# Low parts of the MLP's weights: an accumulating transfer in place of GpSimd's subtraction

## The chip, the cores and the metric

The kernel runs on one core of one Trainium2 chip. The metric is device time in microseconds (us) of one execution; the time before is the median of 2 runs. The engines are named as in the profile: PE (TensorE matmul) and PEld (its weight loads), DVE (VectorE), ACT (ScalarE), POOL (GpSimd) and SP (SyncE). A letter q behind an engine (SPq) stands for its queue, from which transfers are issued.

## What is computed

The reference is one block of a hybrid encoder over 512 tokens and 16 meta tokens (528 in all), 1024 features: a stick-breaking attention and a gated linear attention in parallel, merged by gates, and then a gated MLP with a causal depthwise convolution of width 3. The change touches the MLP alone:

```python
hn = _rmsnorm(h, norm_ffn_pre[l])
up = hn @ w_ffn_up[l]                                   # 1024 x 2816
act = gelu(_causal_dwconv(up, conv_w[l], conv_b[l]))
ffn = (act * (hn @ w_ffn_gate[l])) @ w_ffn_down[l]      # 2816 x 1024
h = h + _rmsnorm(ffn, norm_ffn_post[l])
```

All of it is float32. The kernel multiplies in the format fp32r, which keeps fewer bits, and so each float32 operand x is split exactly into a high part hi (x rounded to fp32r) and a low part lo = x - hi. A product is then three matmuls: hi times hi, hi times lo and lo times hi.

## The kernel before

**Order.** The kernel is written with tiles in named pools. A planner puts the instructions of each engine into one fixed order, by its own estimate of when each can run; on the chip an engine takes its instructions in that order, and each waits for semaphores of the others. SP issues all weight loads from one queue, in order. `issue_after` adds a dependency by hand.

**Weight blocks.** `load_w` (lines 79 to 90) brings one block of at most 1024 weights a partition, 512 KB: SP loads it into `raw` (line 83), ACT rounds it into the high part (line 88), and an engine, POOL unless the call says otherwise, subtracts to give the low part (line 89). The pool `wp` has three `raw` tiles, and two tiles each for the high and the low part (`wh`, `wl`). A caller can give another pool for these two with `into`, or its own places with `hi_out` and `lo_out`.

**The MLP's first half** (lines 922 to 941). A loop over m runs over 22 blocks of 128 of the 2816 columns. Each turn does one up block (`proj`, lines 98 to 110: 8 blocks of rows, three products each, in two column ranges of the tokens), the convolution and GELU on ACT and DVE, one gate block (lines 933 to 939, 24 matmuls of 512 columns), and the split of the product into `fh` and `fl`. Even m take the places of `wp`, odd m those of a second pool, `wx`: four places for 44 weight blocks. For the first two m the two column ranges are apart, so that PE can begin with the tokens that are normed first, and the gate blocks are tied by hand to a step of the norm (`late`, line 932).

**The stage ahead of it** (lines 804 to 915) is the output projection `wo`, its norm, the residual, the second norm and the transposes into `h2h` and `h2l`, one token tile at a time. ACT does squares, rstd steps and the high parts of `h2`; DVE does the gains and half of the low parts, POOL the other half (line 842, through line 204). The loads and splits of the first MLP blocks lie beside it.

**The MLP's second half** (lines 947 to 1006). `down(0, 512, ...)` multiplies `fh` and `fl` with the first 512 columns of the down weights, in blocks of two row blocks, and `down(512, 256, ...)` with the next 256, four row blocks at a time; both go through `wp`. The last 256 columns are loaded whole (lines 988 to 991), in six blocks of four row blocks (the last has two), into `wdh` and `wdl`, and the token tiles then go through them one after the other (lines 993 to 998), so that each tile's final norm and output (lines 999 to 1006) lie beside the next tile's matmuls. In the profile the three are named d, dq and e.

Of the kernel before, what the change touches and what calls it, by code (L numbers as in the profile page):

```python
# [13 lines left out]
ALU = mybir.AluOpType  # L14
# [35 lines left out]
def block_kernel(ctx: ExitStack, tc: tile.TileContext, x, meta_tokens, norm_mix_pre, w_in, w_gk_up, b_gk,  # L50
# [22 lines left out]
    def f32(ap):  # L73
        return ap.bitcast(F32)

# [1 line left out]
    last_raw = [None]  # L77

    def load_w(src, nk, name, hi_out=None, lo_out=None, lo_eng=pool, into=None):
        """A block of at most 1024 weights a partition, and its exact split into two 12-bit parts."""  # L80
        ncol = src.shape[-1]
        raw = wp.tile([P, nk, ncol], F32, tag="raw", name=f"raw_{name}")
        sp.dma_start(raw, src)
        last_raw[0] = raw
        if hi_out is None:
            hi_out = (into or wp).tile([P, nk, ncol], F32R, tag="wh", name=f"wh_{name}", bufs=2)
            lo_out = (into or wp).tile([P, nk, ncol], F32R, tag="wl", name=f"wl_{name}", bufs=2)
        act.copy(hi_out, raw)  # L88
        lo_eng.tensor_tensor(out=lo_out, in0=raw, in1=f32(hi_out), op=ALU.subtract)  # L89
        return hi_out, lo_out  # L90
# [7 lines left out]
    def proj(w, xh, xl, segs, name, apart=False):  # L98
        """Feature-major product over two neighbouring column ranges of xh + xl, in two neighbouring banks."""
        wh, wl = w  # L100
        nk, m = wh.shape[1], wh.shape[2]
        (l0, l1), (_, l2) = segs
        pt = mmt(f"pt_{name}")
        segs = [(pt[:m, 512 - l1 + l0 : 512], l0, l1), (pt[:m, 512 : 512 + l2 - l1], l1, l2)]
        steps = [(k, a, b) for k in range(nk) for a, b in ((wh, xh), (wh, xl), (wl, xh))]
        for grp in ([[s] for s in segs] if apart else [segs]):
            for n, (k, a, b) in enumerate(steps):
                for dst, lo, hi in grp:
                    pe.matmul(dst, a[:, k, :], b[:, k, lo:hi], start=n == 0, stop=n == len(steps) - 1)  # L109
        return pt[:m, 512 - l1 + l0 : 512 + l2 - l1]  # L110
# [3 lines left out]
    def rstd_of(pl, ss, n, name, between=None):  # L114
        """(ss / n + eps) ** -0.5 with a Newton step."""
        shp = list(ss.shape)
        r0 = pl.tile(shp, F32, tag=f"rs_r{shp[1]}", name=f"r0_{name}")
        act.activation(r0, ss, AF.Ln, scale=1.0 / n, bias=epst[: shp[0]])
        last_exp[0] = act.activation(r0, r0, AF.Exp, scale=-0.5)
        v = pl.tile(shp, F32, tag=f"rs_v{shp[1]}", name=f"v_{name}")  # L120
        dve.tensor_scalar(out=v, in0=ss, scalar1=-0.5 / n, scalar2=-0.5 * EPS, op0=ALU.mult, op1=ALU.add)
        if between:
            between()
        a = pl.tile(shp, F32, tag=f"rs_a{shp[1]}", name=f"a_{name}")
        if shp[1] == 1:
            dve.tensor_scalar(out=a, in0=v, scalar1=r0, scalar2=r0, op0=ALU.mult, op1=ALU.mult)
        else:
            dve.tensor_tensor(out=a, in0=r0, in1=r0, op=ALU.mult)
            dve.tensor_tensor(out=a, in0=a, in1=v, op=ALU.mult)
        dve.scalar_tensor_tensor(out=a, in0=a, scalar=1.5, in1=r0, op0=ALU.add, op1=ALU.mult)  # L130
        return a
# [9 lines left out]
    def tables(n):  # L141
        """The activation table set that the next functions are in."""
        return act.add_instruction(mybir.InstLoadActFuncSet(
            act_func_set_id=n, name=nc.get_next_instruction_name(), engine=mybir.EngineType.Activation, ins=[], outs=[]))

    def sigmoid(pl, x, m, nm, bufs=1, tag="lse", out=None):
        """exp(min(x, 0) - ln(1 + exp(-|x|))); m is room for the minimum, or None to read x for it late."""
        e = pl.tile(list(x.shape), F32, tag=tag, name=f"lse{nm}", bufs=bufs)
        act.activation(e, x, AF.Abs)
        if m is not None:  # L150
            dve.tensor_scalar(out=m, in0=x, scalar1=0.0, scalar2=None, op0=ALU.min)
        act.activation(e, e, AF.Exp, scale=-1.0)
        act.activation(e, e, AF.Ln, bias=1.0)
        if m is not None:
            dve.tensor_tensor(out=e, in0=m, in1=e, op=ALU.subtract)
        else:
            dve.scalar_tensor_tensor(out=e, in0=x, scalar=0.0, in1=e, op0=ALU.min, op1=ALU.subtract)
        out = e if out is None else out
        act.activation(out, e, AF.Exp)
        return out  # L160

# [14 lines left out]
    # -1 where row >= column  # L176
# [8 lines left out]
    # =================== normalized input, feature-major, in two parts ===================  # L185
# [13 lines left out]
    def split_g(pl, hi, lo, src, g, nm, lo_eng=dve):  # L199
        """Both parts of src, a block of features after the other, with a gain by feature."""  # L200
        y = pl.tile([P, *src.shape[1:]], F32, tag="yg", name=f"yg{nm}", bufs=4)
        last_yg[0] = dve.tensor_tensor(out=y, in0=src, in1=g.unsqueeze(2).broadcast_to(list(src.shape)), op=ALU.mult)
        last_hi[0] = act.copy(hi, y)
        return lo_eng.tensor_tensor(out=lo, in0=y, in1=f32(hi), op=ALU.subtract)  # L204

    def diagonal(pl, r, n, nm):
        """r on the diagonal: a product with it transposes and scales by token."""
# [4 lines left out]
    with tc.tile_pool(name="p0", bufs=2, side="right") as p0:  # L212
        xts = {i: p0.tile([P, D], F32, name=f"xt{i}", bufs=1) for i in range(1, 5)}
        # the meta tokens, a partition for each block of 128 features, and the gain likewise
# [7 lines left out]
        def warm(n, nm):  # L222
            """Keeps the array's clock up while the first tokens are on their way."""
# [64 lines left out]
        # convolution taps and bias, and the second gain, by feature  # L288
# [40 lines left out]
    # =================== gated linear attention ===================  # L329
    with ExitStack() as pgs:  # L330
        pgc = pgs.enter_context(tc.tile_pool(name="pgc", bufs=1))
        # masks: level masks by compressed query, and the diagonal
# [27 lines left out]
        # log forget gates, token-major  # L360
# [62 lines left out]
        def gla(h, k, q, vT):  # L423
            # cumulative log decay inside chunks
# [12 lines left out]
            # pairs inside a chunk, by the block halves that part them: both factors decay  # L437
            def factors(lv, n, kt):
                """Keys of the first halves of the blocks, in place, and queries of the second halves, packed."""
# [45 lines left out]
            # values, token-major  # L485
# [12 lines left out]
            # queries with the decay since the chunk began, keys with the decay to its end  # L498
# [77 lines left out]
    # =================== stick-breaking attention ===================  # L576
# [4 lines left out]
    with tc.tile_pool(name="pa", bufs=1) as pa:  # L581

        def sb_parts(j, k, q, v):
            """Both parts of a head's keys stacked, against each part of its queries twice; values with both parts side by side."""
# [21 lines left out]
        def logits(dst, w, hd, ks, qs, st):  # L606
            """dst += (k_hi + k_lo).T (q_hi + q_lo)."""
# [3 lines left out]
        def softplus(z, n, rows, nm, i):  # L611
            """softplus of z, in PSUM."""
# [29 lines left out]
        def passed(nm, vp, rows, n, cs, tag):  # L642
            """exp of the sum over a whole key block, for each query, on all partitions."""
# [7 lines left out]
        def sb(j, ks, qh, ql, vs):  # L651
# [3 lines left out]
            # the first and the last 16 tokens: [16, head, (first, last), 16]  # L655
# [13 lines left out]
            # keys 384..511  # L669
# [17 lines left out]
            # out of the first 16 queries  # L687
# [5 lines left out]
            def add_halves(hd, src, t0, n):  # L693
                """The products with both parts of the values, added up."""
# [58 lines left out]
        def gate_sb(j):  # L753
            """A gate, kept where the high part of what it gates will be."""
# [8 lines left out]
    # =================== gates and output projections ===================  # L763
# [3 lines left out]
    # the last two meta tokens: too few for the array, their products are summed over the blocks of 128 rows first  # L767
# [26 lines left out]
    # =================== mixed output, residual, norm ===================  # L794
# [9 lines left out]
    with tc.tile_pool(name="pw", bufs=1) as pw:  # L804
# [7 lines left out]
        def gained(i, pt, hf):  # L812
            """Half of the mixed output of a tile with the gain, and its sum of squares."""
# [12 lines left out]
        def normed(i):  # L826
            """Residual, second norm, and both parts of the result by feature."""
# [16 lines left out]
        def mini():  # L844
            """The same for the last two meta tokens, by feature from the start."""
# [30 lines left out]
        # the first half of the columns for all tokens, then the second one token tile at a time  # L876
# [41 lines left out]
    # =================== gated MLP with the causal convolution ===================  # L918
# [3 lines left out]
    with tc.tile_pool(name="pu", bufs=2) as pu:  # L922
        for m in range(FT):
            pt = proj(load_w(cols(w_up, m * P), KT, f"up{m}", into=wx if m % 2 else None), h2h, h2l, FFNS, f"up{m}", apart=m < 2)
# [7 lines left out]
            with tc.issue_after(late.ins) if m < 2 else ExitStack():  # L932
                wh, wl = load_w(cols(w_gate, m * P), KT, f"ga{m}", into=wx if m % 2 else None)
# [12 lines left out]
    # =================== down projection, norm, residual ===================  # L946
    with tc.tile_pool(name="pd", bufs=1) as pd:
# [40 lines left out]
        for k0 in range(0, FT, 4):  # L988
            nk = min(4, FT - k0)
            load_w(w_down[k0 * P : (k0 + nk) * P, 768:].rearrange("(k p) m -> p k m", p=P), nk, f"e{k0}",  # L990
                   hi_out=wdh[:, k0 : k0 + nk, :], lo_out=wdl[:, k0 : k0 + nk, :])
# [40 lines left out]
```

## Time and profile before

| what | us |
|---|---|
| median of 2 runs (984.88 and 985.22) | 985.05 |
| span of the profiled execution | 983.2 |
| PE busy in it | 958.5 |
| DVE, ACT, POOL busy | 558.8, 461.5, 401.2 |
| first half of the MLP alone on PE | about 626 to 853 |
| second half, to the last matmul | about 853 to 977 |

The profile is one execution, taken by the hardware profiler. Times in the rows of its timeline are us from the start of the span, then the duration, the engine, the line, the operation, the tile written, the tiles read, the shapes and the count of merged instructions; in brackets stands how long the engine sat idle before, and what ended it. The rows of busy time by stretches have the stretch and its length, then busy us (and instruction counts) of PE, PEld, DVE, ACT and POOL, the granted clock of TensorE (1.00 is full), the share of the transfer engines' time, and GB/s. Rows of transfers have the count, the size and the median time from issue to landing. An engine's idle time costs nothing where it is not what the others wait for.

### The profile page before, as it was taken

How to read it: one execution, taken by the hardware profiler on the slowest of the kernel's cores; microseconds unless marked ns; L12 is line 12 of the kernel's file. 1: busy time of each engine (PE TensorE's matmuls, PEld its weight loads, DVE VectorE, ACT ScalarE, POOL GpSimd, SP SyncE). 2: the span in 40 equal slices, each digit the busy share in tenths (PEclk: the TensorE clock that was granted, in tenths of full speed). 3: DMA queues.
4: the chain of work that ended last, by engine and by line, in shares of the span. 5: the costliest groups of instructions: out<-in, count | busy, mean ns of one | idle time of the engine just before them, and what ended most of it. 6: DMA issues, size and time to landing. Idle time of an engine off the chain costs nothing.

```text
span 983.2 us, 17022 instructions
## 1 busy us (share of the span) xinstructions
PE 958.5 (97%) x6918; PEld 895.8 (91%) x6918; DVE 558.8 (57%) x970; ACT 461.5 (47%) x868; POOL 401.2 (41%) x285
## 2 busy tenths in 40 slices
PE   7999999999999998999999899999999999999997
PEld 7999999999999998999998779999988999888997
DVE  6675867767547786787849957444343444300112
ACT  5664645545467574676663244533333333311331
POOL 5523232222244454454545433543443443243460
PEclk9999999999999999999999899999999999999999
DMA  7122221222222222222223441333323323223231
GB/s 212 45 65 65 65 55 54 65 66 60 67 58 72 71 65 65 65 65 66 72 58 112 153 144 43 100 95 91 103 86 92 102 86 95 78 86 102 82 117 65
DMA packets 127552, 81.28 MB, mean 83 GB/s; under 512 B 3680, under 2 KB 120162, under 8 KB 127474
## 3 DMA queue, kind: packets, MB, share of 16 engines
q1 hardware_dynamic: 126082, 76.00, 27.0%
q10 hardware_dynamic: 1392, 4.19, 1.1%
q8 instruction: 54, 0.88, 0.4%
q14 instruction: 24, 0.20, 0.1%
HBM read 78.09 MB, written 2.10 MB: 82 GB/s over the span
## 4 chain that ended last, share of the span: by engine, by line
PE 85%; DVE 8%; issue 2%; ACT 2%; POOL 1%; DMA 1%; SPq 1%; DVEq 0%; POOLq 0%; ACTq 0%
PE pt_up L109 13%; PE ga L938 12%; PE d L965 6%; PE pt_gr L109 5%; PE pt_gv L109 5%; PE pt_go L109 4%; PE pt_mg L109 4%; PE e L998 3%; PE dq L965 3%; PE pt_gk L109 2%; PE pt_sv L109 2%; PE wo L887 2%; PE pt_ms L109 2%; PE pt_gq L109 2%; PE pt_sk L109 2%
## 5 line engine op out<-in xcount | busy, mean ns | idle before, releaser
L89 POOL TENSOR_TENSOR wl_up<-raw_up,wh_up 128x1024 fp32r<-128x1024 f32 x22 | 52.9, 2406 | 70.8 <-ACT wh_up L88 70.8
L89 POOL TENSOR_TENSOR wl_ga<-raw_ga,wh_ga 128x1024 fp32r<-128x1024 f32 x22 | 52.6, 2393 | 56.6 <-ACT wh_ga L88 56.6
L929 DVE SCALAR_TENSOR_TENSOR cy<-pt_up,cw,cy 128x511 f32<-128x511 f32 (+1 forms) x44 | 32.8, 746 | 74.1 <-ACT cy L926 74.1
L109 PE MATMUL pt_up<-h2l,wh_up 128*128 128x256 f32 (+1 forms) x352 | 73.6, 283 | 0.3 <-DVE h2l L204 0.2
L109 PE MATMUL pt_up<-h2h,wh_up 128*128 128x256 f32 (+1 forms) x352 | 73.5, 283 | 0.0
L109 PE MATMUL pt_up<-h2h,wl_up 128*128 128x256 f32 (+1 forms) x352 | 73.3, 282 | 0.0
L938 PE MATMUL ga<-h2l,wh_ga 128*128 128x512 f32 (+1 forms) x192 | 72.2, 376 | 0.0
L938 PE MATMUL ga<-h2h,wl_ga 128*128 128x512 f32 (+1 forms) x192 | 72.1, 375 | 0.0
L938 PE MATMUL ga<-h2h,wh_ga 128*128 128x512 f32 (+1 forms) x192 | 72.1, 376 | 0.0
L89 POOL TENSOR_TENSOR wl_d<-raw_d,wh_d 128x1024 fp32r<-128x1024 f32 (+1 forms) x17 | 39.6, 2332 | 63.7 <-ACT wh_d L88 63.7
L88 ACT CAST wh_up<-raw_up 128x1024 fp32r<-128x1024 f32 x22 | 23.0, 1050 | 85.6 <-PE pt_up L109 76.2
L135 DVE TENSOR_TENSOR fl<-cy,fh 128x512 fp32r<-128x512 f32 x22 | 50.2, 2282 | 15.1 <-ACT fh L134 15.1
L109 PEld LDWEIGHTS pt_up<-h2h,wh_up 128*128 128x128 f32 x352 | 56.9, 189 | 1.7
L109 PEld LDWEIGHTS pt_up<-h2l,wh_up 128*128 128x128 f32 x352 | 55.5, 189 | 0.7 <-DVE h2l L204 0.7
L109 PEld LDWEIGHTS pt_up<-h2h,wl_up 128*128 128x128 f32 x352 | 55.4, 189 | 0.0
L88 ACT CAST wh_d<-raw_d 128x1024 fp32r<-128x1024 f32 (+1 forms) x17 | 17.5, 1029 | 65.8 <-PE d L965 45.1
L940 DVE TENSOR_TENSOR cy<-ga,cy 128x512 f32<-128x512 f32 x22 | 15.2, 691 | 49.0 <-PE ga L938 47.9
L938 PEld LDWEIGHTS ga<-h2h,wl_ga 128*128 128x128 f32 x192 | 36.2, 188 | 7.0
L938 PEld LDWEIGHTS ga<-h2l,wh_ga 128*128 128x128 f32 x192 | 36.2, 188 | 6.2
L938 PEld LDWEIGHTS ga<-h2h,wh_ga 128*128 128x128 f32 x192 | 36.2, 188 | 6.1
L974 DVE TENSOR_TENSOR yb<-d,g3bc 128x512 f32<-128x512 f32 x4 | 2.8, 692 | 61.3 <-ACT dj L977 61.2
L965 PE MATMUL d<-wl_d,fh 128*128 128x512 f32 x88 | 34.8, 396 | 0.0
(522 smaller groups left out, 3234.4 us busy)
## 6 DMA issues: line engine op xcount, KB each, us to landing
raw_up<-in_w_ffn_up_dram SPq DMA_DIRECT2D x22, 512.0 KB, 4.0
raw_ga<-in_w_ffn_gate_dram SPq DMA_DIRECT2D x22, 512.0 KB, 3.9
raw_d<-in_w_ffn_down_dram SPq DMA_DIRECT2D x16, 512.0 KB, 3.5
raw_gv<-in_w_in_dram SPq DMA_DIRECT2D x8, 512.0 KB, 3.9
raw_gr<-in_w_in_dram SPq DMA_DIRECT2D x8, 512.0 KB, 3.8
raw_mg<-in_w_in_dram SPq DMA_DIRECT2D x8, 512.0 KB, 3.9
raw_go<-in_w_gla_out_dram SPq DMA_DIRECT2D x8, 512.0 KB, 4.1
raw_ms<-in_w_in_dram SPq DMA_DIRECT2D x8, 512.0 KB, 3.9
```

The costliest lines, as they stand in the source:

```text
L88: act.copy(hi_out, raw)
L89: lo_eng.tensor_tensor(out=lo_out, in0=raw, in1=f32(hi_out), op=ALU.subtract)
L109: pe.matmul(dst, a[:, k, :], b[:, k, lo:hi], start=n == 0, stop=n == len(steps) - 1)
L135: dve.tensor_tensor(out=lo, in0=src, in1=f32(hi), op=ALU.subtract)
L887: pe.matmul(d0[i], m[k][:, t], w, start=k == 0 and q == 0, stop=k == 7 and q == 2)
L929: dve.scalar_tensor_tensor(out=y[:, d:], in0=pt[:, : SEQ - d], scalar=c, in1=y[:, d:], op0=ALU.mult, op1=ALU.add)
L938: pe.matmul(pg_[:, lo:hi], a[:, k, :], b[:, k, lo:hi], start=lo == 0 and k == 0 and q == 0, stop=k == KT - 1 and q == 2, skip_group_check= ...
L940: dve.tensor_tensor(out=y, in0=pg_, in1=y, op=ALU.mult)
L965: pe.matmul(dsts[i], a[:, k, t], b[:, kk, :], start=k == 0 and q == 0, stop=k == FT - 1 and q == 2)
L974: dve.tensor_tensor(out=yb[:, i, c0 : c0 + n], in0=src, in1=g3bc[:, c0 : c0 + n], op=ALU.mult)
L998: pe.matmul(dst, a[:, k, t], b[:, k, :], start=k == 0 and q == 0, stop=k == FT - 1 and q == 2)
```

## The change

`load_w` gets a parameter `added`. Where it is given, ACT writes minus the high part into the place of the low part, and a transfer issued from POOL's queue adds the weights to it in place, so that raw - hi results as before. With "sbuf" the transfer reads the weights from `raw`, with "dram" it reads them from DRAM a second time. The up and the gate blocks use "sbuf", the last down blocks (e) "dram". All other weights are split as before, the d and dq blocks among them. Comments that the diff also drops are left out here.

```diff
-    def load_w(src, nk, name, hi_out=None, lo_out=None, lo_eng=pool, into=None):
+    def load_w(src, nk, name, hi_out=None, lo_out=None, lo_eng=pool, into=None, added=None):
         ncol = src.shape[-1]
         raw = wp.tile([P, nk, ncol], F32, tag="raw", name=f"raw_{name}")
         sp.dma_start(raw, src)
...
         act.copy(hi_out, raw)
-        lo_eng.tensor_tensor(out=lo_out, in0=raw, in1=f32(hi_out), op=ALU.subtract)
+        if added is None:
+            lo_eng.tensor_tensor(out=lo_out, in0=raw, in1=f32(hi_out), op=ALU.subtract)
+        else:
+            act.mul(lo_out, f32(hi_out), -1.0)
+            pool.dma_start(out=lo_out, in_=raw if added == "sbuf" else src, accum_op=ALU.add)
         return hi_out, lo_out
...
-            pt = proj(load_w(cols(w_up, m * P), KT, f"up{m}", into=wx if m % 2 else None), h2h, h2l, FFNS, f"up{m}", apart=m < 2)
+            pt = proj(load_w(cols(w_up, m * P), KT, f"up{m}", into=wx if m % 2 else None, added="sbuf"), h2h, h2l, FFNS, f"up{m}", apart=m < 2)
...
-                wh, wl = load_w(cols(w_gate, m * P), KT, f"ga{m}", into=wx if m % 2 else None)
+                wh, wl = load_w(cols(w_gate, m * P), KT, f"ga{m}", into=wx if m % 2 else None, added="sbuf")
...
-                   hi_out=wdh[:, k0 : k0 + nk, :], lo_out=wdl[:, k0 : k0 + nk, :])
+                   hi_out=wdh[:, k0 : k0 + nk, :], lo_out=wdl[:, k0 : k0 + nk, :], added="dram")
```

## The prediction

> **What bounds the kernel now.** I read the page first, then busy time by stretches, the chain of work that ended last, what PE waited for, and the timeline of ACT, POOL, SP and PE where the change touches them.
>
> ```profile
> PE 958.5 (97%) x6918; PEld 895.8 (91%) x6918; DVE 558.8 (57%) x970; ACT 461.5 (47%) x868; POOL 401.2 (41%) x285
> ```
> ```profile
> 550.00:600.00 50.00, 48.37 (x232) 39.92 (x231) 37.67 (x67) 20.18 (x49) 21.96 (x10) 0.93 0.47 148
> 600.00:650.00 50.00, 49.84 (x374) 47.49 (x372) 26.09 (x60) 23.84 (x44) 19.42 (x11) 1.00 0.26 74
> 650.00:700.00 50.00, 50.00 (x329) 45.78 (x328) 21.60 (x25) 16.43 (x22) 21.56 (x9) 1.00 0.31 90
> 940.00:983.00 43.00, 36.91 (x312) 36.71 (x311) 11.28 (x32) 9.26 (x28) 10.55 (x5) 0.97 0.24 82
> ```
> ```profile
> 626.34 5.73 PE pt_up L109 x48
> 632.07 5.58 PE ga L938 x24
> ...
> 660.29 5.76 PE pt_up L109 x48
> 666.05 5.57 PE ga L938 x24
> 671.62 5.75 PE pt_up L109 x48
> ...
> 852.84 61.60 PE d L965 x264
> 914.44 31.23 PE dq L965 x264
> 945.67 31.25 PE e L998 x264
> ```
> ```profile
> PE wob L898 <- DVE ml L135: 3.0, 1, 3.0
> PE wob L898 <- DVE hb L817: 1.5, 1, 1.5
> PE pt_up L109 <- DVE h2l L204: 0.2, 1, 0.2
> ```
>
> TensorE is the bound. The stretch rows (columns: span, then busy PE, PEld, DVE, ACT, POOL) show PE busy for all 50 us of a stretch inside the MLP. The chain shows blocks of 5.76 and 5.57 us (a mean of 5.67) end to end, then the down projection without a gap. After 540 us PE waited only for DVE, never for a weight. So the GpSimd subtractions that the change removes lie wholly beside PE. The idle PE time after 550 us is 1.63 + 0.16 + 6.09 = 7.9 us, and the last 6 us of it is the output's tail after the last matmul. Over the whole span idle PE time is 983.2 - 958.5 = 24.7 us, 2.5% of it. A gain above 2% (19.7 us, about what a measurement of this kernel can tell from no change) would need nearly all of that, most of it in stages that the change does not touch.
>
> **The change, part by part.** For 22 up, 22 gate and 6 last down blocks (50 in all) it removes one subtraction on POOL, and adds one pass on ACT and one accumulating transfer issued from POOL's queue. In the steady state of the MLP the rows of one block are:
>
> ```profile
> 654.56 1.05 ACT L88 CAST wh_up<-raw_up 128x1024 fp32r<-128x1024 f32 x1 [4.14 <-PE pt_up L109]
> 655.69 2.41 POOL L89 TENSOR_TENSOR wl_up<-raw_up,wh_up 128x1024 fp32r<-128x1024 f32 x1 [3.34 <-ACT wh_up L88]
> 658.12 0.37 SPq L83 DMA_DIRECT2D raw_ga<-in_w_ffn_gate_dram  x1
> ```
> ```profile
> raw_up<-in_w_ffn_up_dram SPq DMA_DIRECT2D x16, 512.0 KB, 3.9
> q1 hardware_dynamic: 34640, 19.40, 31.5%
> ```
>
> The second fence is from the transfers between 640 and 850 us: issue to landing in the last column, then the queue's share of 16 engines.
>
> *POOL.* About 44 x 2.4 us + 5 x 2.4 + 1.2 (the last block is half a one) = 119 us of subtraction go. PE waited for none of it, so this is worth nothing by itself.
>
> *ACT.* One more pass of 1024 elements: the cast's 1.05 us, in a form with a scale. 44 x 1.05 + 5 x 1.05 + 0.5 = 52 us. In the stretch from 650 to 700 us ACT works 16.43 of 50 us, 3.7 in the 11.33 of two blocks; with 2.1 more it is 5.8, so it fits; the convolution and GELU queued behind it come some 1 to 2 us later, which the PSUM buffers (two of each kind) cover.
>
> *The transfer.* Call D the time from the end of the multiplication to the low part being usable. No row shows an accumulating or a POOL-issued transfer. Nearest are the plain 512 KB loads: 3.9 us here, 3.5 (raw_d) and 4.5 (raw_e) further below. Lower bound 3.5 us, the shortest of these; upper bound 12 us, three plain loads one after the other, since it reads two operands and writes one. I take D = 7: it moves three streams where a load moves two at once, so between one and a half and two plain loads (6 to 8). Even the lower bound is longer than POOL's 2.4 us, so the low part comes later everywhere.
>
> The Trainium skill (DMA: Bandwidth & Descriptors, Anatomy of one DMA — SWDGE (gpsimd) path) gives a fit for GpSimd-issued transfers of 2.0 us plus bytes at 436 GB/s; by it a plain 512 KB would be an estimated 3.2 us, no waits below would appear, and the sum would end near 986 us. No run here shows it, and it has no second operand in it.
>
> *Cover in the steady state.* The cast of block n follows the block that leaves its place (four places, two in each pool), 3 x 5.67 = 17 us before it is needed. Cast 1.05 + multiplication 1.05 + D 7 = 9.1: hidden, 8 us left. The raw tile is now held until the transfer ends, and there are three: load 3.9 + 1.05 + 1.05 + D must stay under 3 x 5.67 = 17.0, so D may reach 11. With D = 7 the cost is 0; that cover is gone above 11.
>
> *Cover at the start of the MLP.* Here the lead is short:
>
> ```profile
> 590.12 1.98 ACT L88 CAST wh_ga<-raw_ga 128x1024 fp32r<-128x1024 f32 x2
> 620.19 1.05 ACT L88 CAST wh_up<-raw_up 128x1024 fp32r<-128x1024 f32 x1 [5.15 <-PE pt_up L109]
> 621.82 1.03 ACT L88 CAST wh_ga<-raw_ga 128x1024 fp32r<-128x1024 f32 x1
> ```
> ```profile
> 600.81 0.28 PE L938 MATMUL ga<-h2h,wl_ga 128*128 128x256 f32 x1
> ```
>
> Block up2: cast from 620.19 to 621.24, multiplication to 622.3, usable at 622.3 + D = 629.3. Its low part is first read as the third product of the block at 626.34, so near 626.8: PE waits 2.5 us (0 at D = 3.5, 7.5 at D = 12). Block ga2: cast after the multiplication and the convolution's first pass, ready near 625.1 + 7 = 632.1, needed at 632.07 + 0.5 + 2.5: hidden. Block ga0: both gate casts end at 592.1, first multiplication at 593.2, usable at 600.2, needed at 600.81: hidden by 0.6 us (at D = 12 a wait of 4.4). Behind the waiting transfer on POOL's queue stand the next transfer and the low parts of h2 of later token tiles.
>
> *ACT and DVE in the second norm.*
>
> ```profile
> 576.93 0.59 ACT L816 ACTIVATE wj<-wo 128x512 f32<-128x512 f32 x1
> 593.65 3.48 DVE L832 SCALAR_TENSOR_TENSOR hb<-hb,a_mix,xr 128x512 f32<-128x512 f32 x2
> 603.63 1.41 DVE L832 SCALAR_TENSOR_TENSOR hb<-hb,a_mix,xr 128x512 f32<-128x512 f32 x2
> ```
> ```profile
> 591.23 4.68 POOL L89 TENSOR_TENSOR wl_ga<-raw_ga,wh_ga 128x1024 fp32r<-128x1024 f32 x2 [0.18 <-ACT wh_ga L88]
> ```
>
> The four multiplications for up0, up1, ga0 and ga1 (4.2 us) fall among the squares and rstd steps that feed the transposes. Against that, the same two DVE instructions took 3.48 us beside POOL's subtraction (from 591.23 to 595.91) and 1.41 without one: some 2 us come back. Net between -2 and +4, and I take +1.
>
> *The tail.* The last six blocks are the narrowest place:
>
> ```profile
> raw_d<-in_w_ffn_down_dram SPq DMA_DIRECT2D x16, 512.0 KB, 3.5
> ...
> raw_e<-in_w_ffn_down_dram SPq DMA_DIRECT2D x5, 512.0 KB, 4.5
> ```
> ```profile
> 938.59 1.05 ACT L88 CAST wdh<-raw_e 128x1024 fp32r<-128x1024 f32 x1 [0.74 <-DMA raw_e<-in_w_ffn_down_dram]
> 940.93 1.05 ACT L88 CAST wdh<-raw_e 128x1024 fp32r<-128x1024 f32 x1 [1.28 <-DMA raw_e<-in_w_ffn_down_dram]
> 943.77 1.05 ACT L88 CAST wdh<-raw_e 128x1024 fp32r<-128x1024 f32 x1 [1.79 <-DMA raw_e<-in_w_ffn_down_dram]
> ...
> 946.67 1.05 ACT L88 CAST wdh<-raw_e 128x1024 fp32r<-128x1024 f32 x1 [1.48 <-DMA raw_e<-in_w_ffn_down_dram]
> ```
> ```profile
> 947.80 3.66 POOL L89 TENSOR_TENSOR wdl<-raw_e,wdh 128x1024 fp32r<-128x1024 f32 x2 [0.50 <-ACT wdh L88]
> ```
>
> The e product goes through 22 row blocks in 31.25 / 4 = 7.81 us for each token tile, from 945.67. Its fifth weight block (rows 16 to 19) is needed at 945.67 + 16/22 x 7.81 = 951.35, and its low part is ready near 950.2: 1.1 us of slack. In the new kernel these raw tiles are free after the cast, because the transfer reads DRAM again: the fifth load can go up to 2.4 us earlier and land near 944.3. ACT then has cast and multiplication of the second, third, fourth and fifth block in a row: 943.77 + 4 x 1.05 = 948.0. With D = 7 the low part is ready at 955.0 and PE waits 3.65 us, once, since the next three token tiles find everything loaded (about 0 at D = 3.5, 8.7 at D = 12). The sixth is half a block and hides behind that.
>
> **Sum.** 0 (steady) + 2.5 (up2) + 1 (ACT and DVE in the norm) + 3.65 (tail) = 7.2 us on the span of 983.2, so 990.4. The median of the runs is 985.05, 1.85 above that span; on that scale 992.2, 0.7% longer.
>
> **The rivals.**
> A, slower: D is near 12, the raw tiles bound the MLP. Then a period is (3.9 + 2.1 + 12) / 3 = 6.0 us for a block in place of 5.67, 0.33 x 40 = 13 us, beside 4.4 + 7.5 + 8.7 + 1 at the places above: 34.6, ending at 1020. It decides from D = 11. Worse, the engines can fill: a plain load holds them for 31.5% of 5.67 = 1.79 us, leaving 3.88, so an accumulating transfer that costs over 2.2 loads of engine time sets the pace itself. At three it is 7.15 us for a block, 1.48 x 42 = 62 us more, near 1054. For it: two reads and a write, issued from a queue that issues no transfer before. Against: 68% of the engines' time is free, and the tiles are whole 4 KB rows where the loads move 512 B pieces. The Trainium skill (Collectives: The Full Stack, The bandwidth ceiling: the fold count and why AG ≠ RS ≠ AR) says that an add in the transfer halves the rate because it needs two source reads; an estimate by that is 2 x 1.79 + 1.79 = 5.4 us for a block, just inside 5.67. No run here shows it.
>
> B, no loss: D is near 3.5 to 4.5, no wait appears, and the 2 us of DVE come back: 983 to 987.
>
> C, the planner orders ACT or POOL otherwise (its order follows its own costs), and a multiplication or a waiting transfer stands in front of a rstd step, a cast or an h2 subtraction. Eight such places at up to 4 us would be 1005 to 1015. For it: the order is re-planned as a whole. Against: in the steady state everything has 8 us of room.
>
> **How the numbers follow.** Forecast 0.53 (its own range 986 to 999), A 0.22 (most of it from 1010 to 1054), B 0.19, C 0.06. Predicted 992. The range 982 to 1020 leaves out the part of A above 1020 (about 0.12) and a small part of B below 982 (0.05). Above 1004.8 lie A and some of C: slower 0.24. Faster than 965 has no mechanism here: 0.01. Within 2%: 0.75.
>
> **What would show it.** Right: the transfers land some 5 to 9 us after the multiplication; PE waits for wl_up once near 626 and for wdl once near 951, with the MLP's blocks at 5.67 us otherwise, and POOL's busy time down by some 119 us. Wrong: a steady block period above 5.7 us with SP waiting for the transfers (A), no PE wait for a low part at all (B), or new PE waits between 575 and 620 for DVE (C).

## The result, and the profile after

The changed kernel takes 996.14 us (median of 2 runs, 995.17 and 997.11) against 985.05: a ratio of 1.0119, 95% interval 1.0083 to 1.0155. It is a little slower, by less than 2%. The forecast was 992.0, in a range of 982 to 1020. The profiled execution has a span of 993.5 us, 10.3 more than the one before.

The page's busy times of the changed kernel, and its busy time by stretches (span, then busy PE, PEld, DVE, ACT, POOL, granted clock, share of the transfer engines, GB/s):

```profile
PE 961.8 (97%) x6918; PEld 898.9 (90%) x6918; DVE 523.8 (53%) x970; ACT 507.7 (51%) x918; POOL 328.2 (33%) x285
```
```profile
550.00:600.00 50.00, 46.80 (x216) 38.95 (x216) 33.25 (x65) 22.36 (x49) 14.37 (x9) 0.91 0.62 164
600.00:650.00 50.00, 49.09 (x369) 46.75 (x368) 20.92 (x56) 28.44 (x51) 8.75 (x9) 1.00 0.52 119
650.00:700.00 50.00, 50.00 (x323) 45.51 (x322) 15.22 (x30) 27.55 (x34) 8.02 (x10) 1.00 0.97 209
940.00:993.00 53.00, 43.34 (x335) 42.23 (x333) 11.27 (x32) 15.45 (x35) 7.62 (x6) 0.90 0.56 128
```

From 650 to 700 us PE is still busy all the time, though the transfer engines went from a share of 0.31 to 0.97. POOL lost 73 us and not 119: the 50 transfers that it now issues are counted as its work, 0.86 to 1.3 us each. The last stretch has a granted clock of 0.90 where it was 0.97.

What PE waited for after 540 us, and the pieces of the chain of waits that show the steady blocks, the one wait at the MLP's start and the end:

```profile
PE e L1003 <- DMA wdl<-in_w_ffn_down_dram: 3.5, 2, 3.0
PE wob L903 <- DVE hb L822: 3.2, 1, 3.2
PE wob L903 <- DVE ml L140: 3.2, 1, 3.2
PE pt_up L114 <- DMA wl_up<-raw_up: 0.9, 1, 0.9
```
```profile
624.60 4.53 DMA wl_up<-raw_up
629.18 5.52 PE pt_up L114 x44
...
662.97 5.76 PE pt_up L114 x48
668.73 5.57 PE ga L943 x24
...
946.43 7.06 DMA raw_e<-in_w_ffn_down_dram
956.27 6.19 DMA wdl<-in_w_ffn_down_dram
962.50 24.41 PE e L1003 x204
```

The steady blocks are 5.76 and 5.57 us as before. New are waits for two kinds of low parts (`wl_up` once, `wdl` twice) and a longer wait of `wob` for `hb` (1.5 before). The end of the chain is what matters most: before, the last 31.25 us were one unbroken run of 264 products of e; now the last 204 of them start only at 962.50, when a low part has landed.

The time can be placed by the starts of the stages. The rows of products by line give the first and the last start of each (the two numbers before the semicolon); in the changed kernel:

```profile
L892 PE MATMUL wo<-wh_oa,mh x32: 391/394/629, 548.4 to 574.8; 128*128 128x512 f32 x32
L114 PE MATMUL pt_up<-h2h,wh_up x352: 276/283/366, 600.5 to 849.2; 128*128 128x256 f32 x168, 128*128 128x258 f32 x8
L970 PE MATMUL d<-wh_d,fh x88: 394/396/397, 855.4 to 916.3; 128*128 128x512 f32 x88
L1003 PE MATMUL e<-wdh,fh x88: 277/282/582, 948.2 to 986.4; 128*128 128x256 f32 x88
```

From the same rows of all kernels, us from first start to first start (for e, from the first start to the last one):

| kernel | norm: wo to up | first half: up to d | e | measured ratio to before, 95% interval |
|---|---|---|---|---|
| before | 48.9 | 254.3 | 30.9 | |
| the change | 52.1 | 254.9 | 38.2 | 1.0119 (1.0083 to 1.0155) |
| `mlp_only` | 53.1 | 254.9 | 30.9 | 1.0053 (1.0034 to 1.0071) |
| `down_only` | 48.6 | 254.2 | 37.5 | 1.0071 (1.0054 to 1.0087) |
| `from_m2` | 48.4 | 256.0 | 30.9 | 1.0014 (1.0000 to 1.0027) |
| `mul_pool` | 48.6 | 255.0 | 30.9 | 1.0021 (1.0008 to 1.0033) |
| `steady_only` | 48.1 | 254.2 | 30.9 | 0.9992 (0.9980 to 1.0004) |
| `filler` | 52.1 | 254.9 | 38.0 | 1.0138 (1.0119 to 1.0157) |
| `early_e` | 51.7 | 254.9 | 30.9 | 1.0038 (1.0022 to 1.0055) |
| `down_sbuf` | 52.9 | 255.0 | 36.8 | 1.0084 (1.0065 to 1.0104) |
| `e_first2` | 48.3 | 254.3 | 35.4 | 1.0057 (1.0041 to 1.0072) |
| `e_last2` | 49.0 | 254.2 | 34.4 | 1.0021 (1.0008 to 1.0033) |
| `both` | 48.6 | 254.2 | 30.9 | 1.0003 (0.9988 to 1.0017) |

d and dq between them take 92.8 or 92.9 us in every one of these. So the change costs 3.2 us in the norm, 0.6 at the start of the MLP and 7.3 in e. That is 11.1; the work ahead of `wo`, which the change does not touch, ended 1.1 us earlier in this execution, the output behind e took 0.3 longer, and 11.1 - 1.1 + 0.3 is the 10.3 of the spans. Such a part ahead of the change differs by up to 4.2 us between single profiled executions (`wo` starts at 550.0 in `e_last2`, at 545.8 in `from_m2`), so stages tell more here than spans do.

**The norm.** ACT and DVE of the changed kernel; the rows of before stand in the prediction (576.93 and 593.65):

```profile
575.59 2.00 ACT L93 ACTIVATE wl_up<-wh_up 128x1024 fp32r<-128x1024 f32 x2
577.49 0.57 ACT L821 ACTIVATE wj<-wo 128x512 f32<-128x512 f32 x1
...
592.73 1.99 ACT L93 ACTIVATE wl_ga<-wh_ga 128x1024 fp32r<-128x1024 f32 x2
594.62 0.19 ACT L124 ACTIVATE r_mix<-r_mix 128x1 f32<-128x1 f32 x1
```
```profile
597.07 1.42 DVE L837 SCALAR_TENSOR_TENSOR hb<-hb,a_mix,xr 128x512 f32<-128x512 f32 x2
```

Two pairs of multiplications stand in ACT's order, the first ahead of the first square, the second between the two steps of an rstd. Counted from each kernel's first `wo` product, the square starts 1.7 us later than before (577.49 - 548.4 against 576.93 - 549.5). DVE's update of `hb` takes 1.42 us in place of 3.48, as foreseen, but starts 4.5 us later by the same count, and so ends 2.5 later.

The chain of waits says which of this counts, and the granted clock (third number from the end) must be read with it. First three pieces of the chain in the change, then the same stretch of time before and in the change:

```profile
575.68 1.91 ACT wl_up L93 x2
...
584.16 2.12 PE wob L903 x8
...
594.01 3.62 PE ht L845 x16
```
```profile
592.00:600.00 8.00, 7.89 (x46) 7.01 (x46) 7.00 (x10) 2.93 (x10) 4.86 (x3) 0.79 0.44 131
```
```profile
592.00:600.00 8.00, 8.00 (x38) 7.46 (x38) 3.82 (x8) 3.78 (x8) 1.77 (x2) 0.57 0.57 107
```

The first pair of multiplications stands in the chain. PE goes on with `wob` after its wait for `hb` at 584.16, 35.76 us behind the first `wo` product; before it was 34.15 (583.65). That is half of the loss. The other half comes between there and the first up product, 16.34 us in place of 14.75. Before, the chain went there through DVE's update of 3.48 us. In the change it runs on PE alone, which was at half clock for 6.8 us (592.9 to 599.7), before for 3.4. The second pair is not in this chain, and DVE's late update does not come from the rstd, which had ended at 594.81: ahead of it DVE had waited until 595.97 for PE's `ht`.

All the profiles of the table agree with this. In the five kernels with four multiplications on ACT the two parts take 35.2 to 35.9 and 16.1 to 17.6 us, and the second has 6.8 or 10.2 us of half clock. In the other eight they take 33.3 to 34.3 and 14.7 or 14.8 us, with at most 3.4 us of half clock. So the longer half clock comes with the multiplications; why it does, no run here shows.

**e.** The fifth weight block (rows 16 to 19) in the changed kernel, on ACT and then on POOL's queue:

```profile
950.92 1.04 ACT L88 CAST wdh<-raw_e 128x1024 fp32r<-128x1024 f32 x1 [1.15 <-DMA raw_e<-in_w_ffn_down_dram]
953.51 0.62 ACT L88 CAST wdh<-raw_e 128x512 fp32r<-128x512 f32 x1 [1.54 <-DMA raw_e<-in_w_ffn_down_dram]
...
954.40 1.56 ACT L93 ACTIVATE wdl<-wdh 128x1024 fp32r<-128x1024 f32 x2
```
```profile
956.27 2.53 POOL L94 DMA_DIRECT2D wdl<-in_w_ffn_down_dram  x2 [4.93 <-ACT wdl L93]
```

It was cast at 950.92, 2.7 us after e began, where before it was 1.2 after. The cast ended at 951.96, but its multiplication began only at 954.40: the planner had put the sixth block's cast in front of it, and that cast waited on ACT for its raw tile until 953.51. The low part landed at about 962.5. In 49 products of 0.118 us e comes to the first product that needs it, so it was due at 948.2 + 5.8 = 954.0, and was 8.5 late. The planner had placed 11 products of the next token tiles ahead (the 60 products before the wait are 49 and 11), which fill 1.3 us of this; 7.2 remain, and e lost 7.3.

PE's long wait in e was an earlier one:

```profile
953.32 0.39 PE L1003 MATMUL e<-wdl,fh 128*128 128x256 f32 x1 [2.96 <-DMA wdl<-in_w_ffn_down_dram]
```

By the count of products ahead of it (13 of the first token tile, 4 of the next), this is the second block (rows 4 to 7). Its multiplication had ended at 943.66, and its low part came 9.6 us later. Then PE waited 0.5 us for the third block, ran at half clock from 954.8 to 961.7, and had about 0.1 us left to wait when it came to the fifth. Whether the late landings or the slow products set the length of e cannot be read from this trace alone; `filler` and `down_only` tell.

### The profile page after: what moved, and what is told of

Read it like the earlier page. It is cut to its first block, busy times and chain, and to the rows that moved or that the text cites. A ratio compares the mean times of both kernels' runs of the same rounds, so it can differ in the third digit from the quotient of the medians.

```text
span 993.5 us, 17138 instructions
## 1 busy us (share of the span) xinstructions
PE 961.8 (97%) x6918; PEld 898.9 (90%) x6918; DVE 523.8 (53%) x970; ACT 507.7 (51%) x918; POOL 328.2 (33%) x285
## 4 chain that ended last, share of the span: by engine, by line
PE 72%; issue 8%; DVE 8%; POOL 5%; DMA 3%; ACT 2%; DVEq 0%; POOLq 0%; ACTq 0%
PE pt_up L114 12%; PE ga L943 11%; PE pt_gr L114 5%; PE pt_gv L114 5%; PE pt_go L114 4%; PE pt_mg L114 4%; POOL wl_d L90 3%; PE pt_ms L114 3%; PE e L1003 2%; PE pt_gk L114 2%; PE pt_sv L114 2%; PE pt_gq L114 2%; PE pt_sk L114 2%; PE pl L478 2%; PE pt_sq L114 2%
## 5 line engine op out<-in xcount | busy, mean ns | idle before, releaser
L94 POOL DMA_DIRECT2D wl_up<-raw_up x22 | 19.1, 869 | 103.8 <-ACT wl_up L93 92.2
L94 POOL DMA_DIRECT2D wl_ga<-raw_ga x22 | 19.0, 869 | 91.2 <-ACT wl_ga L93 91.2
L88 ACT CAST wh_ga<-raw_ga 128x1024 fp32r<-128x1024 f32 x22 | 22.9, 1047 | 25.4 <-PE ga L943 17.2
```

The source lines that it names most:

```text
L94: pool.dma_start(out=lo_out, in_=raw if added == "sbuf" else src, accum_op=ALU.add)
```

## The experiments

The first question was which place costs what. **`mlp_only`** and **`down_only`** each do one half of the change.

```diff
 # mlp_only
-                   hi_out=wdh[:, k0 : k0 + nk, :], lo_out=wdl[:, k0 : k0 + nk, :], added="dram")
+                   hi_out=wdh[:, k0 : k0 + nk, :], lo_out=wdl[:, k0 : k0 + nk, :], added=None)
 # down_only: added=None in the two load_w calls of up and gate
```

> Up and gate blocks by the accumulating transfer, the last down blocks (e) by POOL's subtraction as before. Theory (two narrow places, each priced in the trace of after): only what is lost ahead of the down projection remains, e starts 2.7 us later than before and takes its 31.25 us again, so the time is 2 to 4 us above before (ratio 1.002 to 1.004) and PE waits once near 629 us for wl_up. Rival (the added traffic as such costs, in all of the MLP): 6 to 11 us above before, with block periods above 5.67 us.

> Only the e blocks by the accumulating transfer; up and gate by POOL as before. Theory: the tail loses its 7.3 us without any help of the MLP's transfers: 3.5 us of waits for wdl and some 4 us of half clock behind them, e in 38.5 us, ratio 1.007 to 1.009. Rival (the tail is late because the MLP's transfers pushed the loads back): e in 31 to 33 us, ratio below 1.003.

Measured: 987.52 us and 989.55 us, against 983.31 for the kernel before on the same chip: 4.2 and 6.2 us over. The table shows each loss in its own stage, and together they make 10.4, about the change's 11. So the halves hardly touch each other. Two expectations were missed: `mlp_only` lost a little more than 2 to 4 us, since its norm took 53.1, and in `down_only` no half clock came. There PE waited 5.6 us in four pieces at full clock, and e took 37.5 us all the same.

**`filler`.** After the 2.96 us wait in e, the granted clock was half for 6.8 us. My theory then was that these slow products were part of e's loss. The run puts 14 products whose result nobody reads into that place, so that PE does not fall idle.

```diff
             for k in range(FT):
+                if i == 0 and k == 4:
+                    for _ in range(14):
+                        with tc.issue_after(last_e.ins):
+                            last_e = pe.matmul(pl[0][:, 512:1024], fh[:, 0, 0:128], fh[:, 1, :], start=True, stop=True)
```

> The changed kernel with 14 products more on PE (128x512, into unused columns of e's PSUM, read by nobody) between the 4th and the 5th row block of e's first token tile, some 3.3 us, where PE waited 3.0 us. Theory (the matmuls behind the wait are slow because the granted clock fell to 0.50 during the gap): the clock stays at 1.00 from 946 to 965 us although the same transfers run, matmuls of 256 columns stay at 0.28 us, and the time falls by 2.5 to 4 us below the change although PE does more. Rival (they are slow because the transfer engines are over-full at 1.2 of their time): matmuls of 0.42 us remain, and the time is the change's or up to 1 us more.

The theory fell, and the slow products that its rival expected were not there either. The time was 996.29 us, 13.0 over before on that chip, where the change was 11.1 over. The same stretch, first in the change, then in `filler`, then the end of the chain in `filler`:

```profile
956.00:958.00 2.00, 1.91 (x9) 1.91 (x10) 1.27 (x3) 1.27 (x6) 1.73 (x2) 0.50 0.62 98
```
```profile
956.00:958.00 2.00, 1.05 (x9) 0.85 (x8) 0.15 (x1) 0.00 (x0) 1.16 (x1) 1.00 0.99 147
```
```profile
954.63 5.97 DMA wdl<-in_w_ffn_down_dram
960.64 25.71 PE e L1008 x215
```

The clock stayed at 1.00, and e took 38.0 us all the same: PE now waited where it had worked slowly before, because the last low parts landed no sooner than 12.8 us into e. In the change the slow products were cover for a wait that was coming anyway. With the added products the planner no longer placed the 11 products ahead, which is why 25.71 us were left after the landing and not 24.41.

**`early_e`** takes the tail's lack of time away: the six last blocks are loaded and split beside the fourth to the ninth block of the first down columns, into places that are free then (four in `yb`, two new tiles).

```diff
+            load_w(w_down[k0 * P : (k0 + nk) * P, 768:].rearrange("(k p) m -> p k m", p=P), nk, f"e{k0}", hi_out=wdh[:, k0 : k0 + nk, :],
+                   lo_out=wdl[:, k0 : k0 + nk, :], added="dram", raw=places[j], after=last_split)
...
+                if not c0 and 3 <= k0 // step < 9:
+                    early_e(k0 // step - 3)
...
+        places = [yb[:, b, :].rearrange("p (k m) -> p k m", k=4) for b in range(4)]
+        places += [pd.tile([P, 4, QC], F32, name="re4"), pd.tile([P, 2, QC], F32, name="re5")]
```

> The changed kernel, but the six raw e blocks have places of their own (four in yb, two new), are loaded early in the down projection, and their cast, multiplication and transfer stand behind those of the 4th to 9th d block. Nothing else changes. Theory (the tail's loss is lateness of the last transfers): no wait for wdl, e in 31.3 us at full clock, 6.5 to 7.5 us below the change, so 2 to 4 above before. Rival (an accumulating transfer beside the d blocks costs as much there: POOL's queue is held, wl_d comes late): PE waits for wl_d and most of the 7 us stays.

Measured: 986.32, 3.0 over before, and the chain ends in one piece as it did before the change:

```profile
946.17 31.25 PE e L1012 x264
```

The transfers took 8.3 us here as well (median from issue to landing), and cost nothing, since they had the time.

**`from_m2`, `mul_pool` and `steady_only`** take the start apart. The first leaves feature blocks 0 and 1 to the subtraction, the third blocks 0 to 3; both do the last down columns by subtraction. `mul_pool` keeps all the transfers of up and gate, but lets GpSimd write minus the high part for blocks 0 and 1.

```diff
 # from_m2 (steady_only: m >= 4), for up and gate alike
-added="sbuf"
+added="sbuf" if m >= 2 else None
 # mul_pool
+            if added == "pool":
+                pool.tensor_scalar(out=lo_out, in0=f32(hi_out), scalar1=-1.0, scalar2=None, op0=ALU.mult)
+            else:
+                act.mul(lo_out, f32(hi_out), -1.0)
...
+added="sbuf" if m >= 2 else "pool"
```

> Up and gate blocks from feature block 2 on by accumulating transfer; blocks 0 and 1 of both, and the last down columns, by GpSimd's subtraction as before. Theory (the second norm pays for the multiplications that stand on ScalarE ahead of its own work: two pairs of 2.0 us, at 575.6 and at 592.7 in the profile after, some 1.6 us lost by each): without these four multiplications the stretch from the first wo product to the first up product is 48.9 us as before (52.1 with the change), only the wait of block 2 at the start of the MLP is left (up to 0.9 us), and the time is 0 to 1 us over the kernel before. Rival (the loss comes from the transfers beside the norm or from the order that the planner chose): the stretch stays over 50.5 us and the time 2.5 us or more over before.

> Up and gate blocks from feature block 4 on by accumulating transfer, everything else by GpSimd's subtraction. Theory (in the steady part a low part has about 17 us of lead, and the transfers there cost nothing): blocks of 5.76 and 5.57 us, no wait for wl_up or wl_ga, the time within 0.7 us of the kernel before. Rival (fuller DMA engines, a share of 0.88 in place of 0.31, do cost something in the steady part or after it): 2 us or more over before.

> As the run with up and gate alone added, but for feature blocks 0 and 1 GpSimd writes minus the high part in place of ScalarE; the transfers of all 44 blocks stay, the last down columns are split by subtraction. Theory (the second norm lost its 3.2 us to the multiplications standing on ScalarE ahead of squares and rstd steps): the stretch from the first wo product to the first up product falls from 53.1 us to 48.5 to 50.5, and the time is 0.5 to 2 us over before, with block 2's wait left. Rival (the norm loses it to the transfers themselves, landing late or beside its own, or to DVE running beside GpSimd): the stretch stays at 51.5 us or more, the time 3 us or more over before.

Measured against 983.26, 983.26 and 983.30: `from_m2` 983.90, `steady_only` 982.86, `mul_pool` 984.86. In all three the norm is back at 48.1 to 48.6 us. `mul_pool` decides between the two reasons that were left: every transfer is there, only ACT is spared, and the norm loses nothing. GpSimd pays more for the same work, 5.53 us for two blocks, where it has the time:

```profile
572.42 5.53 POOL L94 TENSOR_SCALAR wl_up<-wh_up 128x1024 fp32r<-128x1024 f32 x2 [5.42 <-ACT wh_up L88]
```
```profile
573.18 0.59 ACT L824 ACTIVATE wj<-wo 128x512 f32<-128x512 f32 x1
```

The first square on ACT (second fence) now starts 27.1 us after the first `wo` product (546.1), before 27.4. `from_m2` lost more at block 2 than I had expected, a wait of 1.4 us where I had put at most 0.9, and 1.7 us in its stage. `steady_only` shows the steady part by itself: 36 added blocks, no loss.

**`down_sbuf`** asked whether reading the DRAM a second time is the slow part. Its expectation calls it a run with the last down columns alone; in fact up and gate are added in it too, as in the change, and only the source of the last six transfers differs, so it is to be held against the change.

```diff
-                   hi_out=wdh[:, k0 : k0 + nk, :], lo_out=wdl[:, k0 : k0 + nk, :], added="dram")
+                   hi_out=wdh[:, k0 : k0 + nk, :], lo_out=wdl[:, k0 : k0 + nk, :], added="sbuf")
```

> Only the last down columns by accumulating transfer, and the source is the raw tile in SBUF in place of a second reading of the DRAM. Theory (the tail is bound by what the DMA engines get through while raw loads and added transfers share them, and a raw tile of which there are three is now held until its transfer has landed): an e stage of 37 us or more, the time 5 us or more over before. Rival (the second reading of the DRAM is the slow part: 8.3 us from issue to landing, while up and gate took 5.6 and 6.2 from SBUF): transfers of about 6 us, an e stage of 32 to 35 us, and 1 to 4 us over before.

```profile
wdl<-raw_e POOLq DMA_DIRECT2D x5, 512.0 KB, 6.1
```
```profile
L94 POOL DMA_DIRECT2D wdl<-raw_e x6: 859/859/874, 938.6 to 960.3; - x6
```

Both expectations were half right. Measured: 991.16 us, 7.9 over before. The transfers are shorter from SBUF, 6.1 us from issue to landing against 8.3, and yet e takes 36.8 us, 1.4 less than in the change. The raw tiles are held longer, and the last transfer is issued at 960.3, 11.5 us into e, where in the change it is 8.8 (957.0 - 948.2). What one gained, the other took.

**`e_first2` and `e_last2`** tell apart two readings of e's loss: lead (each low part is ready later than by subtraction) and full transfer engines (a share above 1 from 942 to 956 us in the change). Only the first two, or only the last two, of the six blocks are added; the other weights are all subtracted.

```diff
-added="dram")
+added="dram" if k0 < 8 else None)     # e_last2: k0 >= 16
```

> Of the six low parts of the last down columns only the first two (rows 0 to 7 of 22) by accumulating transfer, the other four and all of up and gate by GpSimd's subtraction. Theory of lead (what counts is when the last low parts land; each added one is ready some 9 us later than by subtraction): only the second block can be late, cast 7.1 us ahead of the e stage, landed some 4 to 5 us into it, due 1.4 us into it: a wait of 2.5 to 3.6 us, an e stage of 33 to 34.5 us, 2 to 4 us over before. Theory of full DMA engines (raw loads and added transfers together are more than the engines get through between 938 and 962): a third of the added bytes leaves them free, no wait over 1 us, e stage under 32 us, within 1 us of before.

> Of the six low parts of the last down columns only the last two (rows 16 to 21 of 22) by accumulating transfer, the rest and all of up and gate by GpSimd's subtraction. Theory of lead: the fifth block is cast 1.1 us into the e stage, multiplied and issued by about 4, landed at 10 to 12, the sixth a little later, due at 5.7 and 7.1: an e stage of 35.5 to 37.5 us, 4.5 to 6.5 us over before, nearly the loss of all six. Theory of full DMA engines: two transfers in place of six, raw loads as early as before, an e stage under 33 us, less than 2 us over before.

The ends of their chains, `e_first2` first:

```profile
939.85 9.54 DMA wdl<-in_w_ffn_down_dram
949.43 31.49 PE e L1003 x251
```
```profile
949.95 6.04 DMA wdl<-in_w_ffn_down_dram
956.03 24.99 PE e L1003 x196
```

The times were 988.50 and 985.15 us, 5.7 and 2.4 over before (982.78), and e was 4.5 and 3.5 us longer. Both runs lost more than full engines allowed, but neither met the forecast of lead in full: the first lost more, the second less. (The profile of `e_last2` is of the longest of its 12 executions, 989.17.)

`e_last2` shows lead by itself. Its transfer had no raw load beside it and took 6.0 us, and PE still waited 1.8 us, after 19 products of the next token tile that the planner had placed ahead, 2.2 us of cover. In `e_first2` the wait is 2.7 us, at the second block, as expected; but there the engines' load decides as well. Beside raw loads, with a share of the transfer engines of 1.06 to 1.19 from 940 to 948 us, the transfer took 9.5 us. With 6.0 it would have landed at 945.9, and the wait began only at 946.7. So the two readings go together: full engines make the landing later, and the lead decides whether that costs.

And here the clock did cost. After the wait both ran at half clock with nothing left to wait for (first `e_first2`, then `e_last2`):

```profile
948.00:952.00 4.00, 2.57 (x12) 2.57 (x13) 1.60 (x4) 3.25 (x10) 2.80 (x3) 0.68 0.10 29
```
```profile
956.00:960.00 4.00, 3.97 (x22) 3.97 (x23) 0.06 (x1) 0.47 (x2) 0.00 (x0) 0.61 0.24 37
```

The 251 products that were left in `e_first2` took 31.49 us; at 31.25 / 264 they would have taken 29.7. So 1.8 us are the clock's, which with the wait of 2.7 makes the 4.5.

**`both`** puts together what cost nothing: up and gate from block 4 on, and the early last blocks.

> Up and gate from feature block 4 on by accumulating transfer, and the six last down blocks loaded, cast, multiplied and added beside row blocks 4 to 9 of the down projection's first columns. Theory (the losses are at the start of the MLP and at the tail alone, and both are a matter of place): within 1 us of the kernel before, e stage 30.9 us. Rival (the transfers have a cost wherever they are): 2 us or more over before.

Measured: 983.09 against 983.26, no difference. 42 of the 50 subtractions are gone, GpSimd is busy for 339.5 us in place of 401.2, and nothing is gained by it. No version tried here is faster than the kernel before.

## Why the prediction was right, and where its terms were off

The outcome (a small loss, within 2%) and the places (the second norm, block up2, the low parts of e) were right, but of the three terms none had its size: 1 + 2.5 + 3.65 = 7.2 was forecast, 3.2 + 0.6 + 7.3 = 11.1 came. The time lies 4.1 us over the forecast, and inside its range. That the first two errors, 2.2 too little and 1.9 too much, cancel is luck; what is left is the tail's.

- *POOL*, worth nothing: right. `both` and `steady_only` take most of the subtractions away and gain nothing.
- *Cover in the steady state*, cost 0: right (`steady_only`). The numbers inside it moved against each other: the raw loads take 5.9 to 7.2 us in place of 3.9, the added transfers less than the 7 that I took.

```profile
raw_up<-in_w_ffn_up_dram SPq DMA_DIRECT2D x22, 512.0 KB, 5.9
raw_ga<-in_w_ffn_gate_dram SPq DMA_DIRECT2D x22, 512.0 KB, 7.2
wl_up<-raw_up POOLq DMA_DIRECT2D x22, 512.0 KB, 5.6
wl_ga<-raw_ga POOLq DMA_DIRECT2D x22, 512.0 KB, 6.2
```
```profile
q0 software_dynamic: 5301, 19.29, 53.5%
q1 hardware_dynamic: 37851, 20.90, 34.7%
```

- The second fence is of the transfers from 640 to 850 us, the stretch that the prediction used; q0 is GpSimd's queue. An accumulating transfer holds the engines for 53.5% of 5.67 = 3.0 us a block, and it may hold them for 3.88 (rival A's bound of 2.2 loads): it is 1.7 plain loads of 1.79. Rival A was nearer than the steady blocks let one see: together the two queues use 88% of the engines. The Trainium skill (Collectives: The Full Stack, The bandwidth ceiling: the fold count and why AG ≠ RS ≠ AR) says of a reduce-scatter that its add needs two source reads and so has half the rate; the 1.7 agrees with its direction and nearly with its size. The fit of the Trainium skill (DMA: Bandwidth & Descriptors, Anatomy of one DMA — SWDGE (gpsimd) path), which gave an estimated 3.2 us, is far from the 5.6 and 8.3 measured; it has no second operand in it.
- *Cover at the start of the MLP*: the mechanism was right, D too long. The low part of up2 was usable 4.9 us after its multiplication (624.31 to 629.18), the wait 0.9 us and not 2.5.
- *ACT and DVE in the second norm*: +1 was too small, 3.2 is inside the -2 to +4 that I gave. The 2 us of DVE came back as foreseen. The step that failed was to set them off against the multiplications: what DVE saved was not saved on the chain. The first pair cost its 1.6 us there in full, and behind it the chain ran on PE at half clock, another 1.6 us that no term had. `mul_pool` shows that without the multiplications on ACT nothing of the loss remains.
- *The tail*: the mechanism, low parts that come too late, was right, and the size was half of the 7.3 that e lost. PE's wait near 951, which was named as a sign, came, but by luck: it was for the second block, for which D was 9.6. For the fifth block D was 7, as taken (its multiplication ended near 955.4, the low part came at 962.5), and still it was 8.5 us late where I had 3.65. The two sentences that failed are "the fifth load can go up to 2.4 us earlier" and "ACT then has cast and multiplication of the second, third, fourth and fifth block in a row". By these the cast would have begun 0.4 us after e's first product; it began at 2.7. The fifth load was issued at 944.11, 4.1 us ahead of e against 3.4 before, when GpSimd's subtraction of the last dq block ended (944.08), and it landed later since the raw loads beside the added transfers took 6.8 us in place of 4.5:

```profile
raw_e<-in_w_ffn_down_dram SPq DMA_DIRECT2D x5, 512.0 KB, 6.8
```

- And the multiplication did not follow the cast but stood 2.4 us behind it, with another cast waiting in front. 2.3 + 2.4 is nearly the 4.8 that was missing. In place of these two sentences the runs show loads that are slower beside the added transfers: the share of the transfer engines was above 1 from 942 to 956 us, and in `mlp_only`, where no e block is added, the same loads took 3.5 us.
- *Rival C* (another order by the planner) came true in part. Its sign, a longer wait for DVE between 575 and 620, is there (`hb`, 3.2 us in place of 1.5), and the multiplications ahead of the first square and the cast ahead of the fifth multiplication are of its kind; but these are two places and not eight. *Rival B* is excluded by the waits.
- *The clock*: a clock that falls was in no part of the prediction, though the trace of before has a wait of 3.0 us and a granted clock of 0.50 from 548 to 552 us behind it. It goes with half of the norm's loss and with part of that of `e_first2` and `e_last2`; the change's loss in e it did not decide.

## What to carry to other kernels

Work that moves from an engine with slack to a queue has to be costed by lead: from the moment the input is there to the moment the output is usable, against the moment it is due, for the first and the last blocks of each stage and not for the steady ones. The loads beside the new transfers are to be costed at their new, slower landing, and on an in-order engine every added instruction, and every instruction that waits in front of it, counts wherever a short chain of small steps runs through that engine. Where PE is at 100% and never waits for what is removed, there is nothing to win; the best version here (`steady_only`, `both`) only comes back to even.

## What the runs showed of the hardware

- An accumulating transfer of 512 KB from GpSimd's queue took 5.6 to 6.2 us from issue to landing with SBUF as its source, 8.3 with DRAM (6.0 where no raw load ran beside it, 9.5 where one did), and each issue held GpSimd for 0.86 (SBUF) to 1.3 us (DRAM).
- The granted clock of TensorE fell to half after some idle gaps and not after others: after 1.8 us in `e_last2`, 2.1 in `down_sbuf`, 2.7 in `e_first2` and 3.0 in the change, but not in `down_only`, which waited 2.6 us and three times more within 12 us, nor in `filler`. In the norm it also fell long after a gap: before, PE's wait ended at 583.65 and the half clock began at 594.4. The Trainium skill (TensorE: Matmul & The Clock Gate, Part 1: The HAM clock gate) has a free-running window of some 3.4 us. The lengths agree with it, 3.4 us of half clock in `e_last2`, `down_sbuf` and `e_first2` and 6.8 in the change. Its rule there, no idle gaps of PE above some 3.4 us, does not hold here as a limit: shorter gaps were followed by half clock.
